# Dilated attention's product groups tied to their last operand, and the exchange's second product moved to the dense PSUM pool

## Chip, cores, metric

One core of a Trainium2 chip runs the whole kernel in one launch. The metric is the device time of the kernel in microseconds (us); the time before is the median of three runs. TensorE is called PE here, VectorE DVE, ScalarE ACT, GpSimd POOL and SyncE SP. A "row" of an instruction order is one instruction, or a run of equal ones.

## The reference

A transformer block over 2048 positions of width 1024, in float32. What matters here is the attention part and the dense products around it (cut):

```python
DILATED_PAIRS = ((128, 1), (512, 4), (2048, 16))     # (window, dilation)

def dilated_branch(q, k, v, slopes, window, dilation):
    ...
    s = jnp.einsum('bdhnqe,bdhnke->bdhnqk', qb, kw).astype(jnp.float32) * (E ** -0.5)
    ...
    s = jnp.where(valid, s + alibi, -jnp.inf)
    m = jnp.max(s, axis=-1, keepdims=True)
    p = jnp.exp(s - m)
    den = jnp.sum(p, axis=-1, keepdims=True)
    o = jnp.einsum('bdhnqk,bdhnke->bdhnqe', p, vw.astype(jnp.float32)) / den
    lse = (m + jnp.log(den))[..., 0]
    ...

def dilated_attention_group(q, k, v):
    ...                                               # the three branches
    weights = jax.nn.softmax(jnp.stack(lses, axis=0), axis=0)
    return jnp.einsum('gbsh,gbshe->bshe', weights, jnp.stack(outs, axis=0))

def reference(...):
    ...
    h = rms_norm(x, norm1_g[l]) * (1 + sc1) + sh1
    proj = h @ w_in[l]                                # input projection
    ...                                               # gated linear attention, dilated attention
    x = x + g1 * (mixed @ w_out[l])
    h = rms_norm(x, norm2_g[l]) * (1 + sc2) + sh2
    u = causal_depthwise_conv(h @ w_up[l], conv_w[l], conv_b[l])
    u_gate, u_val = jnp.split(u, 2, axis=-1)
    x = x + g2 * ((jax.nn.silu(u_gate) * u_val) @ w_down[l])
```

## The kernel before

The 2048 positions are four chunks of 512. Dense products (input projection, output projection, up, down) are each split into three float32r products that add up in one PSUM bank: lines L301, L302 and L303 of `mm3`, 128x512 each, 24 in a row for one output tile of most products and 12 for one of the down projection. A dense product takes its bank from the pool `psg` (four banks, `pg()`), and DVE or ACT reads it out.

Beside this dense work runs the mixing of a chunk: `mix(c)` is two calls of `gla` and four of `attn(c, hp)`, one for each pair of heads. There are 16 calls of `attn` in all, called steps 0 to 15 here (steps 0 to 3 are chunk 0). All of mixing takes its PSUM banks from the pool `psa` (four banks, `pa()`). `run` interleaves the two generators in program order (`beside`): chunk 0's mixing with the input projection, the mixing of chunks 1 to 3 with the output projection and feed-forward part of the chunk before. The order on each engine is then made by a scheduler, which walks its own model of the time and places an instruction on its engine when operands and buffers are ready in that model; each engine executes its rows in that order. A pool gives its buffers out in the order in which the program asks for them.

One step of attention, in the order of the code:

- The scores of the three branches: dilation 16 (L814), 4 and 1 (`scores`, L779, first with `qf`, then with `qn`). A group in `scores` is eight products on four `psa` banks; a bank holds two of them for one head, and the two heads' products alternate. DVE adds the bias and takes the maximum (`TTR`, L785, eight a group); ACT takes the exponentials with their sums (L789, eight a group).
- The exchange, which brings the maxima and sums of the branches to one layout. DVE makes `xm` (L841), PE multiplies it by the constant `x1` (L844, called the x1 product), then a chain of small operations runs on DVE with one exponential on ACT (L846, L847, L849, L851, L852, L853, L854 to L857), which ends in a second `xm` (L860). PE multiplies that by the constant `x4` (L868, the exchange's second product, called the x4 product here). DVE reads it (L870, L871).
- Scaling of the probabilities by DVE (L864 for dilation 4, L875 for dilation 1) and their transposition by PE (`turn`, L799: four transposes into a bank, then one copy by ACT or DVE in turn, L178 and L180); the transposes of dilation 16 stand ahead of the x4 product in the code.
- The products with the values (L896, L901), a last transposition (L916), the sum (L919).

Of the kernel before, what the change touches and what calls it, by code (L numbers as in the profile page):

```python
# [131 lines left out]
class K:  # L132
    def __init__(self, tc, A, ctx):
        self.tc, self.nc, self.A, self.ctx = tc, tc.nc, A, ctx
        pool = lambda name, bufs, **kw: ctx.enter_context(tc.tile_pool(name=name, bufs=bufs, **kw))
        self.const = pool("const", 1)
        self.wraw = pool("wraw", 2)
        self.whi = pool("whi", 4)
        self.wlo = pool("wlo", 4)
        self.hp = pool("hp", 10)  # L140
        self.gp = pool("gp", 5)
        self.xp = pool("xp", 8)
        self.up = pool("up", 2)
        self.tmp = pool("tmp", 2)
        self.at = pool("at", 1)
        self.dr = pool("dr", 1, space=DRAM)
        self.psg = pool("psg", 4, space=PSUM)
        self.psa = pool("psa", 4, space=PSUM)
        self.evac = 0
        self.loads = []  # L150
        self.hist = []

# [10 lines left out]
    def pa(self, name="psa"):  # L163
        return self.psa.tile([P, T], F32, name="psa")

    def pg(self):
        return self.psg.tile([P, T], F32, name="psg")

# [5 lines left out]
    def copy(self, out, in_):  # L174

        self.evac += 1
        if self.evac % 2:
            self.nc.scalar.copy(out, in_)  # L178
        else:
            self.nc.vector.tensor_copy(out, in_)  # L180

    def consts(self):
        nc, A = self.nc, self.A
# [123 lines left out]
    def ada_setup(self):  # L307
        nc, c = self.nc, self.A["c"]
        self.cond = self.const.tile([P, 1024], F32, name="cond")
        nc.sync.dma_start(self.cond, bass.AP(tensor=c.tensor, offset=c.offset, ap=[[0, P], [1, 1024]]))  # L310
        self.n1 = self.cload("norm1_g", [P, KD])
        self.n2 = self.cload("norm2_g", [P, KD])
        self.ba = self.cload("b_ada", [P, 48])
        self.ones = self.const.tile([P, P], F32, name="ones")
        nc.vector.memset(self.ones, 1.0 / 1024)
        self.eps = self.const.tile([P, 1], F32, name="eps")
        nc.vector.memset(self.eps, EPS)
        th = self.at.tile([P, 1024], F32, name="big", bufs=4)
        tanh = nc.scalar.activation(th, self.cond, AF.Tanh, scale=0.5)
        pre = nc.scalar.preload_act_table_set("natural_log_exp_and_others")  # L320
        self.tc.add_manual_dep(pre.ins, tanh.ins.name, mybir.DependencyInfo(mybir.DependencyClass.Sync, mybir.DependencyReason.DATA))
        nc.vector.scalar_tensor_tensor(self.cond, th, 1.0, self.cond, op0=ALU.add, op1=ALU.mult)
        self.mod = self.const.tile([P, 48], F32, name="mod")
        self.G1 = self.const.tile([P, KD], F32, name="G1")
        self.G2 = self.const.tile([P, KD], F32, name="G2")

    def after(self, inst):

# [122 lines left out]
    def proj(self, c, hs, hook=None, done=()):  # L451
# [58 lines left out]
        def wide(b):  # L510

            pss = [self.pg() for _ in range(4)]
            for j in range(4):
                w = self.weights("w_tokw", b, j)
                order = [(i, s) for i in range(2) for s in range(4)]
# [6 lines left out]
                    self.mm3(pss[s], [(h[:, tk], l[:, tk])], w[i:i + 1], i == 0 and j == 0, True)  # L522
                if j < 3:
                    yield
            for s in range(4):
                off = b and put_off
                st = stage("y0" if off else None)
# [213 lines left out]
    def attn(self, c, hp):  # L741
# [30 lines left out]
        def scores(q, key, z0, bias, outs, g):  # L772
# [3 lines left out]
            for i in range(4):  # L776
                z = z0(i)
                for hh in range(2):
                    nc.tensor.matmul(at(i, hh, z), q[H[hh], i * P:(i + 1) * P], key(H[hh], i, z), start=True, stop=True, skip_group_check=True)  # L779
            for i in range(4):  # L780
                z = z0(i)
                for hh in range(2):
                    TTR(outs[hh][:, i, z:], at(i, hh, z), bias[:, z:], mx[:, hh, g, i:i + 1])

        TTR = lambda out, i0, i1, acc: nc.vector.tensor_tensor_reduce(out, i0, i1, 1.0, -3.0e38, ALU.add, ALU.max, acc)  # L785

        def soft(t, hh, g, i, lo, hi):
            h = 2 * hp + hh
# [2 lines left out]
        nm = self.at.tile([P, 2, 3, 4], F32, name="nm", bufs=2)  # L791
        slp = self.C("slp")[:, 24 * hp:24 * hp + 24].rearrange("p (a g i) -> p a g i", a=2, g=3)

        def turn(n, b0, part, to):

            for hh in range(2):
                ps = self.pa()
                for i in range(b0, 4):
                    nc.tensor.transpose(ps[:n, i * P:(i + 1) * P], part(S[hh], i), self.C("id"))  # L799
                self.copy(to(S[hh]), ps[:n, b0 * P:].rearrange("p (r n) -> p r n", n=P))  # L800

        def exps(g, part):

# [57 lines left out]
        for hh in range(2):  # L861
            for i in range(4):
                z = 0 if c else P
                nc.vector.tensor_scalar(s4[hh][:, i, z:], s4[hh][:, i, z:], f[:, hh, 1, i:i + 1], None, op0=ALU.mult)  # L864
        turn(nk, 0, lambda t, i: t[0][:, i * nk:(i + 1) * nk], lambda t: t[0][:nk].rearrange("p (r n) -> p r n", n=P))
        yield
        ps = self.pa()
        nc.tensor.matmul(ps[:, 0:32], self.C("x4"), xm.rearrange("p a b r -> p (a b r)"), start=True, stop=True)  # L868
        xm = self.at.tile(x4, F32, name="xm", bufs=2)[:, 0:2]
        nc.vector.tensor_tensor(xm, ps[:, 0:32].rearrange("p (a b r) -> p a b r", b=4, r=4), self.C("s1")[:, None, None, :].to_broadcast(x2), op=ALU.mult)  # L870
# [1 line left out]
        for hh in range(2):  # L872
            for i in range(4):
                z = 0 if (c or i) else P
                nc.vector.tensor_scalar(sn[hh][:, i, z:], sn[hh][:, i, z:], f[:, hh, 2, i:i + 1], None, op0=ALU.mult)  # L875

        def weigh(out, g):

# [4 lines left out]

        cols = lambda r4, hh: slice((2 * r4 + hh) * 64, (2 * r4 + hh + 1) * 64)
        for z in (P, 0) if c else (P,):
            turn(P, 0, lambda t, i: t[1][:, i, z:z + P], lambda t: t[1][:, :, z:z + P])
        yield
        for z in (P, 0):
            b0 = 0 if (c or z) else 1
            turn(P, b0, lambda t, i: t[2][:, i, z:z + P], lambda t: t[2][:, b0:, z:z + P])  # L890
        yield
        O16 = self.pa()
        for hh in range(2):
# [269 lines left out]
```

## Time and profile before

| | |
|---|---|
| median of the runs | 2615.92 us (2615.84 to 2618.74) |
| profiled execution | 2615.61 us; span of its instructions 2613.8 us |
| busy | PE 98%, DVE 74%, ACT 49%, POOL 17% |
| chain of work that ended last | PE 95% of the span |
| mean granted PE clock | 0.995 |
| DMA | 405.10 MB, mean 155 GB/s |

A row of a group reads: line, engine, operation, tile written and tiles read, sizes, number; then busy time in us and mean ns of one; then the idle time of the engine just before these instructions and what ended it. A row of the timeline reads: start and length in us, engine, line, operation, number of instructions merged, and in brackets the idle time before. A float32 matmul leaves two records in the trace, so eight products stand as x16. Successive matmuls overlap, so a row's length is longer than the step from one start to the next; a step of 0.227 us from one 128x512 product to the next is the dense pace.

### The profile page before, as it was taken

Reading aid. Unit: us, or ns where it says so; the run is one execution under the profiler, and the core shown is the slowest. Engines: PE = TensorE matmul, PEld = TensorE weight load, DVE = VectorE, ACT = ScalarE, POOL = GpSimd, SP = SyncE. Lnnn points to the kernel's source line nnn. Section 1 sums busy time; section 2 is a strip of 40 time slices with the busy share of each in tenths; the row PEclk is TensorE's granted clock in tenths of the full one; section 3 lists DMA queues with packets and bytes.
Section 4 is the critical chain, followed back from the end, with each engine's and each line's share of the span. In section 5 each row is a group of like instructions: output and inputs, shape, how many; then the busy total and the mean of one; then the engine's idle time right before and its main releaser. Section 6 shows DMA issues by size and latency. Waiting matters only on the chain.

```text
span 2613.8 us, 46823 instructions
## 1 busy us (share of the span) xinstructions
PE 2563.5 (98%) x18152; PEld 2105.6 (81%) x18152; DVE 1922.3 (74%) x4075; ACT 1288.8 (49%) x2622; POOL 440.9 (17%) x812
## 2 busy tenths in 40 slices
PE   5999999999999999999999999999999999999999
PEld 3887888788788888887788888878888888788887
DVE  7578886767778777776888777679777775766665
ACT  4566556666554444543555444345445453433332
POOL 1343342312210000012100000310000002200001
PEclk9999999999999999999999999999999999999999
DMA  8766575655632344345423444643344435432222
GB/s 297 254 220 222 186 249 178 212 173 190 236 121 94 114 129 133 120 147 209 141 92 117 140 132 140 241 148 106 115 142 138 134 115 185 153 100 98 97 98 85
DMA packets 164992, 405.10 MB, mean 155 GB/s; under 512 B 19985, under 2 KB 62754, under 8 KB 163490
## 3 DMA queue, kind: packets, MB, share of 16 engines
q0 software_dynamic: 88128, 308.59, 35.1%
q1 hardware_dynamic: 76642, 93.51, 11.3%
q8 instruction: 143, 2.34, 0.4%
q14 instruction: 79, 0.65, 0.1%
HBM read 339.12 MB, written 62.91 MB: 154 GB/s over the span
## 4 chain that ended last, share of the span: by engine, by line
PE 95%; DMA 1%; DVE 1%; ACT 1%; issue 1%; SPq 0%; POOL 0%; POOLq 0%; DVEq 0%; ACTq 0%
PE psg L301 27%; PE psg L302 27%; PE psg L303 27%; PE psa L799 3%; PE psa L779 2%; PE psa L901 2%; PE psa L635 2%; PE psa L896 1%; PE psa L708 1%; PE psa L814 1%; PE psa L707 1%; DVE wada L348 0%; PE psa L712 0%; DMA qf<-q 0%; DMA k_norm_g_sb<-in_k_norm_g_dram 0%
## 5 line engine op out<-in xcount | busy, mean ns | idle before, releaser
L302 PE MATMUL psg<-hlo,whi 128*128 128x512 f32 x1992 | 783.9, 394 | 8.4 <-DVE hlo L447 8.0
L301 PE MATMUL psg<-hhi,whi 128*128 128x512 f32 x1992 | 783.0, 397 | 9.0 <-ACT hhi L445 6.4
L303 PE MATMUL psg<-hhi,wlo 128*128 128x512 f32 x1992 | 781.9, 393 | 0.7 <-DVE wlo L236 0.7
L235 ACT CAST whi<-wraw 128x1024 fp32r<-128x1024 f32 (+1 forms) x391 | 410.5, 1051 | 482.1 <-PE psg L302 386.2
L236 DVE TENSOR_TENSOR wlo<-wraw,whi 128x1024 fp32r<-128x1024 f32 (+1 forms) x391 | 478.2, 1223 | 205.2 <-ACT whi L235 196.5
L301 PEld LDWEIGHTS psg<-hhi,whi 128*128 128x128 f32 x1992 | 375.1, 189 | 96.0 <-ACT hhi L445 12.0
L302 PEld LDWEIGHTS psg<-hlo,whi 128*128 128x128 f32 x1992 | 376.1, 189 | 88.8 <-DVE hlo L447 11.3
L303 PEld LDWEIGHTS psg<-hhi,wlo 128*128 128x128 f32 x1992 | 376.3, 189 | 81.5 <-issue 2.0
L301 PE MATMUL psg<-ghi,whi 128*128 128x512 f32 x744 | 294.3, 397 | 0.1
L302 PE MATMUL psg<-glo,whi 128*128 128x512 f32 x744 | 292.6, 393 | 0.8 <-DVE glo L945 0.8
L303 PE MATMUL psg<-ghi,wlo 128*128 128x512 f32 x744 | 291.8, 392 | 0.7 <-DVE wlo L236 0.7
L229 POOL DMA_DIRECT2D wraw<-in_w_up_dram x176 | 93.2, 529 | 988.5 <-DVE wlo L236 814.3
L1019 DVE SCALAR_TENSOR_TENSOR x<-psg,mod,x 128x512 f32<-128x512 f32 x192 | 143.3, 749 | 118.8 <-PE psg L303 118.3
L301 PE MATMUL psg<-whi,hhi 128*128 128x512 f32 (+2 forms) x512 | 172.4, 344 | 0.6 <-ACT stg L531 0.5
L302 PE MATMUL psg<-wlo,hhi 128*128 128x512 f32 (+2 forms) x512 | 173.0, 339 | 0.0
L303 PE MATMUL psg<-whi,hlo 128*128 128x512 f32 (+2 forms) x512 | 172.6, 341 | 0.0
L301 PEld LDWEIGHTS psg<-ghi,whi 128*128 128x128 f32 x744 | 139.6, 188 | 33.5 <-issue 4.1
L302 PEld LDWEIGHTS psg<-glo,whi 128*128 128x128 f32 x744 | 139.8, 188 | 31.3 <-issue 2.6
L303 PEld LDWEIGHTS psg<-ghi,wlo 128*128 128x128 f32 x744 | 139.7, 188 | 30.4 <-DVE wlo L236 1.1
L789 ACT ACTIVATE big<-big,nm 128x256 f32<-128x256 f32 (+1 forms) x256 | 122.4, 480 | 34.1 <-DVE nm L804 34.1
L974 ACT ACTIVATE y<-psg,conv_b_sb,conv_w_sb 128x512 f32<-128x512 f32 x176 | 136.0, 775 | 3.0 <-PE psg L303 1.7
L975 DVE SCALAR_TENSOR_TENSOR y<-psg,conv_w_sb,y 128x511 f32<-128x511 f32 x176 | 130.7, 743 | 3.0 <-ACT y L974 2.8
(237 smaller groups left out, 3608.4 us busy)
## 6 DMA issues: line engine op xcount, KB each, us to landing
wraw<-in_w_up_dram POOLq DMA_DIRECT2D x176, 512.0 KB, 3.6
wraw<-in_w_down_dram POOLq DMA_DIRECT2D x88, 512.0 KB, 3.6
wraw<-in_w_ch_dram POOLq DMA_DIRECT2D x44, 512.0 KB, 4.4
v<-v SPq DMA_DIRECT2D x68, 256.0 KB, 5.2
wada<-in_w_ada_dram POOLq DMA_DIRECT2D x64, 256.0 KB, 4.6
wraw<-in_w_tokw_dram POOLq DMA_DIRECT2D x32, 512.0 KB, 4.4
wraw<-in_w_out_dram POOLq DMA_DIRECT2D x32, 512.0 KB, 4.8
sq<-in_xT_dram POOLq DMA_DIRECT2D x48, 256.0 KB, 5.0
```

The lines of the kernel that those rows point to most:

```text
L229: self.dq.dma_start(raw[:, :n], src)
L235: nc.scalar.copy(hi[:, :n], raw[:, :n])
L236: nc.vector.tensor_tensor(lo[:, :n], raw[:, :n], hi[:, :n].bitcast(F32), op=ALU.subtract)
L301: nc.tensor.matmul(ps, wh, hh, start=first and k == 0, stop=False, skip_group_check=shared)
L302: nc.tensor.matmul(ps, wh, hl, start=False, stop=False, skip_group_check=shared)
L303: self.lastmm = nc.tensor.matmul(ps, wl, hh, start=False, stop=k == n - 1, skip_group_check=shared)
L635: nc.tensor.matmul(sp[j:j + w, o + n * w:o + (n + 1) * w], kh[R, k0:k0 + w], qh[R, q0:q0 + w], start=True, stop=True)
L789: nc.scalar.activation(t[:, lo:hi], t[:, lo:hi], AF.Exp, bias=nm[:, hh, g, i:i + 1], scale=2.0 ** -(h + 1), accum_out=dn[:, hh, g, i:i + 1])
L799: nc.tensor.transpose(ps[:n, i * P:(i + 1) * P], part(S[hh], i), self.C("id"))
L974: nc.scalar.activation(y, ps, AF.Identity, bias=self.cb[:, b:b + 1], scale=self.cw[:, 2, b:b + 1])
L975: nc.vector.scalar_tensor_tensor(y[:, 1:], ps[:, :T - 1], self.cw[:, 1, b:b + 1], y[:, 1:], op0=ALU.mult, op1=ALU.add)
L1019: nc.vector.scalar_tensor_tensor(x1, ps, self.mod[:, 40 + cb:41 + cb], x1, op0=ALU.mult, op1=ALU.add)
```

## The change

- `tie(inst, to)` adds a dependency: `inst` begins after `to` has completed. The first product of a group in `scores` is tied to the last `TTR` before it. The first transpose of dilation 4's probabilities is tied to the last of their scalings, and the first of dilation 1's to the last of theirs and to the last copy of the transposes before.
- The x4 product takes its bank by `px()`: from `psg`, the dense pool, unless a `wide` product has all four of that pool's banks open at that place of the program; then from `psa` as before.

```diff
+    def px(self):
+
+        return self.pa() if self.wide_open else self.pg()
...
         self.evac += 1
         if self.evac % 2:
-            self.nc.scalar.copy(out, in_)
-        else:
-            self.nc.vector.tensor_copy(out, in_)
+            return self.nc.scalar.copy(out, in_)
+        return self.nc.vector.tensor_copy(out, in_)
...
+    def tie(self, inst, to):
+
+        self.tc.add_manual_dep(inst.ins, to.ins.name, mybir.DependencyInfo(mybir.DependencyClass.Sync, mybir.DependencyReason.DATA))
...
             pss = [self.pg() for _ in range(4)]
+            self.wide_open = True
...
+            self.wide_open = False
...
-                    nc.tensor.matmul(at(i, hh, z), q[H[hh], i * P:(i + 1) * P], key(H[hh], i, z), start=True, stop=True, skip_group_check=True)
+                    mm = nc.tensor.matmul(at(i, hh, z), q[H[hh], i * P:(i + 1) * P], key(H[hh], i, z), start=True, stop=True, skip_group_check=True)
+                    if i == hh == 0:
+
+                        self.tie(mm, last["ttr"])
...
-        TTR = lambda out, i0, i1, acc: nc.vector.tensor_tensor_reduce(out, i0, i1, 1.0, -3.0e38, ALU.add, ALU.max, acc)
+        last = {}
+
+        def TTR(out, i0, i1, acc):
+            last["ttr"] = nc.vector.tensor_tensor_reduce(out, i0, i1, 1.0, -3.0e38, ALU.add, ALU.max, acc)
...
-        def turn(n, b0, part, to):
+        def turn(n, b0, part, to, wait=()):
 
             for hh in range(2):
                 ps = self.pa()
                 for i in range(b0, 4):
-                    nc.tensor.transpose(ps[:n, i * P:(i + 1) * P], part(S[hh], i), self.C("id"))
-                self.copy(to(S[hh]), ps[:n, b0 * P:].rearrange("p (r n) -> p r n", n=P))
+                    tr = nc.tensor.transpose(ps[:n, i * P:(i + 1) * P], part(S[hh], i), self.C("id"))
+                    if wait:
+
+                        for w in wait:
+                            self.tie(tr, w)
+                        wait = ()
+                last["copy"] = self.copy(to(S[hh]), ps[:n, b0 * P:].rearrange("p (r n) -> p r n", n=P))
...
-                nc.vector.tensor_scalar(s4[hh][:, i, z:], s4[hh][:, i, z:], f[:, hh, 1, i:i + 1], None, op0=ALU.mult)
+                last["s4"] = nc.vector.tensor_scalar(s4[hh][:, i, z:], s4[hh][:, i, z:], f[:, hh, 1, i:i + 1], None, op0=ALU.mult)
...
-        ps = self.pa()
+        ps = self.px()
         nc.tensor.matmul(ps[:, 0:32], self.C("x4"), xm.rearrange("p a b r -> p (a b r)"), start=True, stop=True)
...
-                nc.vector.tensor_scalar(sn[hh][:, i, z:], sn[hh][:, i, z:], f[:, hh, 2, i:i + 1], None, op0=ALU.mult)
+                last["sn"] = nc.vector.tensor_scalar(sn[hh][:, i, z:], sn[hh][:, i, z:], f[:, hh, 2, i:i + 1], None, op0=ALU.mult)
...
-            turn(P, 0, lambda t, i: t[1][:, i, z:z + P], lambda t: t[1][:, :, z:z + P])
+            turn(P, 0, lambda t, i: t[1][:, i, z:z + P], lambda t: t[1][:, :, z:z + P], (last["s4"],) if z else ())
...
-            turn(P, b0, lambda t, i: t[2][:, i, z:z + P], lambda t: t[2][:, b0:, z:z + P])
+            turn(P, b0, lambda t, i: t[2][:, i, z:z + P], lambda t: t[2][:, b0:, z:z + P], (last["sn"], last["copy"]) if z else ())
```

In the changed file the lines lie further down: the dense products are L305 to L307, the scores L789, the transposes L815, the x1 product L865 and the x4 product L889, with `xm` from L862 and L881.

How the rows stand, at three places. First PE in step 4 (the first of chunk 1, beside the down projection of chunk 0). The numbers behind a name count the tiles in the order in which the program makes them. Before, around the x1 product `psa_9872`:

```order
L303 MATMUL psg_9915<-ghi_8915,wlo_9719 128x512
L844 MATMUL psa_9872<-xm_9828,consts_sb_442 128x64
L799 MATMUL psa_9897<-consts_sb_442,s16_9546 64x128 x4
L799 MATMUL psa_9903<-consts_sb_442,s16_9547 64x128 x4
L301 MATMUL psg_9915<-ghi_9079,whi_9718 128x512
L302 MATMUL psg_9915<-glo_9081,whi_9718 128x512
L303 MATMUL psg_9915<-ghi_9079,wlo_9719 128x512
L301 MATMUL psg_9966<-ghi_8608,whi_9718 128x512
```

and, 32 dense products after the x1 product, around the x4 product `psa_9929`:

```order
L301 MATMUL psg_10092<-ghi_8758,whi_9786 128x512
L302 MATMUL psg_10092<-glo_8760,whi_9786 128x512
L868 MATMUL psa_9929<-xm_9887,consts_sb_442 128x32
L799 MATMUL psa_9942<-consts_sb_442,big_9674 128x128 x4
L799 MATMUL psa_9948<-consts_sb_442,big_9675 128x128 x3
```

Now:

```order
L307 MATMUL psg_9915<-ghi_9079,wlo_9719 128x512
L865 MATMUL psa_9872<-xm_9828,consts_sb_442 128x64
L815 MATMUL psa_9897<-consts_sb_442,s16_9546 64x128 x4
L815 MATMUL psa_9903<-consts_sb_442,s16_9547 64x128 x4
L889 MATMUL psg_9929<-xm_9887,consts_sb_442 128x32
L305 MATMUL psg_9966<-ghi_8608,whi_9718 128x512
L306 MATMUL psg_9966<-glo_8610,whi_9718 128x512
```

Before, the dense tiles 9966, 10010 and 10092 begin ahead of tile 9929; now 9929 stands in the dense pool's sequence, and 9966 and all later dense tiles begin behind it. Between the x1 and the x4 product there are the eight transposes and no dense product.

Second, PE in step 2 (chunk 0, beside the input projection), from the last scores to the x4 product. Now:

```order
L789 MATMUL psa_5939<-kw_5674,qn_5672 128x256
L789 MATMUL psa_5940<-kw_5674,qn_5672 128x256
L593 MATMUL psa_6036<-consts_sb_442,gl_5630 16x128 x4
L600 MATMUL psa_6044<-gw_459,glr_6041 128x256 x2
L600 MATMUL psa_6053<-gw_459,glr_6041 128x256 x2
L865 MATMUL psa_6065<-xm_6034,consts_sb_442 128x64
L815 MATMUL psa_6090<-consts_sb_442,s16_5716 32x128 x4
L815 MATMUL psa_6096<-consts_sb_442,s16_5717 32x128 x4
L486 MATMUL psa_6148<-sqr_6141,blk_464 128x512
L487 MATMUL psa_6148<-sqr_6142,blk_464 128x512
L889 MATMUL psg_6166<-xm_6080,consts_sb_442 128x32
L305 MATMUL psg_6197<-hhi_5568,whi_5873 128x512
```

Before, the same x1 product stood in the middle of tile 6197, with dense products on both sides:

```order
L301 MATMUL psg_6197<-hhi_5610,whi_5873 128x512
L590 MATMUL psa_6044<-gw_459,glr_6041 128x256 x2
L590 MATMUL psa_6053<-gw_459,glr_6041 128x256 x2
L844 MATMUL psa_6065<-xm_6034,consts_sb_442 128x64
L799 MATMUL psa_6090<-consts_sb_442,s16_5716 32x128 x4
L302 MATMUL psg_6197<-hlo_5612,whi_5873 128x512
L303 MATMUL psg_6197<-hhi_5610,wlo_5874 128x512
```

From the last score to the x1 product 46 dense products stood before and none stands now.

Third, DVE in step 13 (chunk 3, beside the up projection of chunk 2), from the chain's first rows on. Now:

```order
L867 TENSOR_TENSOR xm<-psa,consts_sb 128x64
L868 TENSOR_REDUCE md<-xm 128x4x4
L870 TENSOR_REDUCE M<-md 128x8
L240 TENSOR_TENSOR wlo<-wraw,whi 128x1024
L872 TENSOR_TENSOR f<-md,M 128x24
L184 COPY s_20343<-psa 128x512
L996 SCALAR_TENSOR_TENSOR y_20706<-psg,conv_w_sb,y_20706 128x511
L999 SCALAR_TENSOR_TENSOR y_20706<-halo,conv_w_sb,y_20706 128x1
L1007 SCALAR_TENSOR_TENSOR th<-th,y_20631 128x512
L873 TENSOR_TENSOR f<-f,consts_sb 128x24
```

Before:

```order
L846 TENSOR_TENSOR xm<-psa,consts_sb 128x64
L847 TENSOR_REDUCE md<-xm 128x4x4
L236 TENSOR_TENSOR wlo<-wraw,whi 128x1024
L180 COPY s_20343<-psa 128x512
L849 TENSOR_REDUCE M<-md 128x8
L975 SCALAR_TENSOR_TENSOR y_20631<-psg,conv_w_sb,y_20631 128x511
L978 SCALAR_TENSOR_TENSOR y_20631<-halo,conv_w_sb,y_20631 128x1
L991 TENSOR_TENSOR glo<-y_20585,ghi 128x512
L851 TENSOR_TENSOR f<-md,M 128x24
```

In both, rows that read dense results or split weights stand between the rows of the chain; which ones stand there has shifted by about one dense tile.

More of the change, by code (lines that the diff above doesn't have):

```diff
@@ L524, in wide @@
                     yield
+            self.wide_open = False
             for s in range(4):
```

## The prediction

> **What bounds the kernel now.** I read first the busy times and the shares of the chain that ended last, then the busy time of the long middle of the run, then single steps of attention in the timeline.
>
> ```profile
> PE 2563.5 (98%) x18152; PEld 2105.6 (81%) x18152; DVE 1922.3 (74%) x4075; ACT 1288.8 (49%) x2622; POOL 440.9 (17%) x812
> PE 95%; DMA 1%; DVE 1%; ACT 1%; issue 1%; SPq 0%; POOL 0%; POOLq 0%; DVEq 0%; ACTq 0%
> 400.00:2200.00 1800.00, 1790.05 (x13718) 1465.55 (x13718) 1353.52 (x3132) 915.45 (x2052) 262.32 (x484) 1.00 0.45 148
> ```
>
> PE is the bound. In the 1800 us of the third row (length, then busy time of PE, PEld, DVE, ACT and POOL, granted clock) it stands still for 10 us in all. So a change can win only by making PE's own rows cheaper, up to those 10 us, and every new wait of PE lengthens the run by its whole length, since no slack is left to take it up. PE can be kept busy because the attention's waits are filled with dense products. The question is whether they still are.
>
> The exchange of step 4 shows what is filled (start, length, engine, line):
>
> ```profile
> 937.99 0.33 PE L844 MATMUL psa<-xm,consts_sb 128*128 128x64 f32 x2
> 938.15 1.04 PE L799 MATMUL psa<-consts_sb,s 128*64 128x128 f32 x8
> 939.22 0.22 DVE L846 TENSOR_TENSOR xm<-psa,consts_sb 128x64 f32<-128x64 f32 x1
> 940.04 0.68 DVE L180 COPY s<-psa 64x512 f32<-64x512 f32 x1
> 940.64 0.17 DVE L852 TENSOR_TENSOR f<-f,consts_sb 128x24 f32<-128x24 f32 x1
> 940.74 0.74 DVE L1019 SCALAR_TENSOR_TENSOR x<-psg,mod,x 128x512 f32<-128x512 f32 x1
> 940.84 0.22 ACT L853 ACTIVATE f<-f 128x24 f32<-128x24 f32 x1 [1.47 <-DVE f L852]
> 941.40 0.17 DVE L854 TENSOR_TENSOR md<-md,f 128x24 f32<-128x24 f32 x1
> 942.27 0.20 DVE L860 TENSOR_TENSOR xm<-f,consts_sb 128x32 f32<-128x32 f32 x1
> 942.38 2.19 DVE L864 TENSOR_SCALAR big<-big,f 128x256 f32<-128x256 f32 x8
> 946.31 0.31 PE L868 MATMUL psa<-xm,consts_sb 128*128 128x32 f32 x2
> ```
>
> The x4 product's operand is written by L860, which ends at 942.47, 4.48 us after the x1 product began; the x4 product runs at 946.31. Nobody waits in these 8.3 us, because 32 dense products fill them.
>
> **A. The x4 product in the dense pool: waits.** The pool hands out its buffers in program order. With the x4 product's tile in that sequence, no dense product that comes later in the program may begin before it. In the changed order of PE the dense products between the x1 and the x4 product number, from step 0 to 15: 0, 58, 0, 0, 0, 24, 0, 9, 2, 0, 0, 0, 24, 0, 0, 0; none had fewer than 32 before. Steps 1, 5 and 12 keep cover; in 13 steps PE holds little but the x1 product and eight transposes, 937.99 to 939.19 above, 1.2 us, and then waits. Behind the x4 product in PE's queue stand all the dense rows.
>
> The wait is the latency of the chain less that work. The chain alone: 0.33 us of the x1 product and 942.47 − 939.22 = 3.25 us from L846 to L860 (a copy and an L1019 are in it), 3.6 us. DVE takes its rows in order, and in the changed order more rows stand within the chain: 9 splits of weights, 31 rows of the feed-forward's or projection's read-outs.
>
> ```profile
> L236 DVE TENSOR_TENSOR wlo<-wraw,whi 128x1024 fp32r<-128x1024 f32 (+1 forms) x391 | 478.2, 1223 | 205.2 <-ACT whi L235 196.5 <-PE psg L303 3.2 <-PE psa L479 0.2
> L976 DVE SCALAR_TENSOR_TENSOR y<-psg,conv_w_sb,y 128x510 f32<-128x510 f32 x176 | 130.9, 744 | 0.7
> L986 DVE SCALAR_TENSOR_TENSOR th<-th,y 128x512 f32<-128x512 f32 x88 | 60.7, 689 | 35.9 <-ACT th L985 35.9
> L979 DVE SCALAR_TENSOR_TENSOR y<-halo,conv_w_sb,y 128x2 f32<-128x2 f32 x132 | 28.0, 212 | 0.0
> 1047.64 0.39 PE L301 MATMUL psg<-hhi,whi 128*128 128x512 f32 x1
> 1049.71 0.39 PE L301 MATMUL psg<-hhi,whi 128*128 128x512 f32 x1
> ```
>
> They cost 9 × 1.223 = 11.0, 31 × 0.72 (between the 0.744 and 0.689 of the two middle rows) = 22.3, and seven of L979's kind 1.5: 34.8 us. Between the two PE rows lie nine steps, 0.23 us each; the 11 dense products that stand in steps 7 and 8 cover 2.5 us, two small groups (L478, L479) 0.7. So 13 × 3.6 + 34.8 − 13 × 1.2 − 3.2 = **63 us**. Step by step (0, 2, 3, 4, 6, 7, 8, 9, 10, 11, 13, 14, 15): 7.7, 2.9, 5.6, 2.4, 5.8, 5.2, 5.7, 5.2, 3.6, 2.4, 6.9, 6.9, 2.4. The low end is the chain with none of those rows in its way, 46.8 − 15.6 − 3.2 = 28: once PE stands still it makes nothing new for DVE to read. The high end takes the latencies from the x1 product to the end of L860 as they were in these 13 steps; the first and last:
>
> ```profile
> 439.68 0.33 PE L844 MATMUL psa<-xm,consts_sb 128*128 128x64 f32 x2
> 447.90 0.19 DVE L860 TENSOR_TENSOR xm<-f,consts_sb 128x32 f32<-128x32 f32 x1
> 2134.68 0.33 PE L844 MATMUL psa<-xm,consts_sb 128*128 128x64 f32 x2
> 2142.95 0.19 DVE L860 TENSOR_TENSOR xm<-f,consts_sb 128x32 f32<-128x32 f32 x1
> ```
>
> 8.4 and 8.5 us, 102 over all 13: 102 − 15.6 − 3.2 = 83. I take 63, from the rows as they now stand in DVE's order.
>
> **B. The x1 product: waits.** It moves forward as well, since the x4 product behind it now holds the dense rows. Between the last dilation-1 score and the x1 product stood at least 41 dense products in every step; now step 2 has none, step 9 20, step 10 22, steps 14 and 15 33, the others 42 or more. What they covered is the maximum, the exponentials and L841:
>
> ```profile
> 1606.65 2.00 PE L779 MATMUL psa<-kw,qn 64*128 64x256 f32 x16
> 1618.01 0.23 DVE L841 TENSOR_TENSOR xm<-md,consts_sb 128x64 f32<-128x64 f32 x1 [3.38 <-ACT big L789]
> 563.57 1.14 PE L779 MATMUL psa<-kw,qn 64*128 64x256 f32 x8
> 572.06 0.23 DVE L841 TENSOR_TENSOR xm<-md,consts_sb 128x64 f32<-128x64 f32 x1
> L590 PE MATMUL psa<-gw,glr 17*128 17x256 f32 x32 | 8.0, 387 | 0.0
> ```
>
> From the end of the scores at 1608.65 to 1618.24 are 9.6 us (step 11); in step 2, 564.71 to 572.29, 7.6. Waits: 9.6 − 20 × 0.23 = 5.0; 4.5; twice 2.0; and in step 2 7.6 less some 2.0 of small groups (four products of L590 and four transposes) 5.6. Sum **19 us**. Low: two fewer rows of L236's kind in the way, 2.4 less in each, 8; high: two more in each, 31.
>
> **C. The clock after a wait.** Two waits of PE stand in the trace with what followed:
>
> ```profile
> 617.17 0.88 PE L814 MATMUL psa<-kt,qf 64*32 64x32 f32 x64 [2.89 <-DMA qf<-q]
> 617.20:620.50 3.30, 3.30 (x76) 3.23 (x77) 1.15 (x17) 1.21 (x8) 0.00 (x0) 0.50 0.89 327
> 1748.60 0.26 PE L635 MATMUL psa<-pt 64*32 64x32 f32 x6 [1.90 <-issue]
> 1748.60:1752.00 3.40, 3.40 (x20) 2.80 (x20) 3.40 (x8) 2.34 (x5) 2.65 (x5) 1.00 0.59 174
> ```
>
> After 2.89 us without work the next 3.3 us ran at a granted clock of 0.50, which costs half of them, 1.65 us; after 1.90 us the clock stayed at 1.00. Of the waits above ten of A (2.9 and longer) and three of B are as long as the first: 13 × 1.65 = **21 us**. Low: only the five longest, about twice 2.89 us and more (steps 0, 6, 8, 13 and 14), 8; high: two such stretches for each, 43.
>
> [...]
>
> **D. The ties: groups joined.** Where half a group of scores waited for a bank, dense products stood between the halves; the first product of a tied group waits until all four banks are read, and its eight run together. Step 6 shows both kinds:
>
> ```profile
> 1044.51 1.13 PE L779 MATMUL psa<-kw,qf 64*128 64x256 f32 x8
> 1045.58 0.50 PE L301 MATMUL psg<-hhi,whi 128*128 128x512 f32 x1
> 1045.91 0.40 PE L302 MATMUL psg<-hlo,whi 128*128 128x512 f32 x1
> 1046.24 1.14 PE L779 MATMUL psa<-kw,qf 64*128 64x256 f32 x8
> 1047.30 0.50 PE L303 MATMUL psg<-hhi,wlo 128*128 128x512 f32 x1
> 1052.52 2.00 PE L779 MATMUL psa<-kw,qn 64*128 64x256 f32 x16
> 1054.44 0.50 PE L301 MATMUL psg<-hhi,whi 128*128 128x512 f32 x1
> ```
>
> Start to start, the halves take 1.07 + 1.06 us, the whole 1.92: 0.21 saved. A dense product beside a switch takes 0.33 in place of 0.23, on both sides, which saves another 0.20: 0.41 a join. Runs of scores fall from 51 to 36: nine joins of two halves in chunks 1 to 3 (3.7), one of three pieces (some 0.8 to 1.5), five in chunk 0 (2.0); runs of transposes fall from 92 to 52, priced at 0.8 in all, since joined transposes save the switch alone and many runs only touch other attention rows. Sum **−8 us**, bounds −4 (scores of chunks 1 to 3) and −12 (a 0.10 switch on every transposes' join too). The ties themselves make no new wait: before dilation 4's transposes stand 21 to 27 dense products, at least 4.8 us, against eight scalings that take 2.19 us together (the L864 row), and 22 to 33 more before dilation 1's. POOL, SP and the DMAs they issue keep their order but for small shifts; DMA queues are not what PE waits for.
>
> **Sum.** 63 + 19 + 21 − 8 = +95 to the profiled execution's 2615.6 us (0.3 under the median): about 2711 us. I take 2712.
>
> **Rivals.**
> The queue drains. While PE stands still, DVE may already be through the rows that I put into the chain, and only the lone chain is left: A 28, B 8, C 12 (waits of 2.4 us lie midway between 1.90 and 2.89, so half of 13 fall), D −8: +40, 2656 us. For it: DVE is busy 74% only; against: those rows stand ahead of the chain's in DVE's own order and read products that PE ends just before it waits.
> The clock stays low. Each wait costs two half-clock stretches, and the latencies are the measured ones: 83 + 19 + 43 − 8 = +137, 2753 us. For it: two waits a step lie within 10 us of each other.
> Other side: the chain is ready before the eight transposes end. That needs a latency under about 1.2 us at each x4 product; then A and C vanish, B with them, and D's −8 is left: 2608 us. The shortest latency in the trace is step 4's 4.48, so little speaks for it.
> The change does nothing: the bank's pool rarely limits and the moved products cost and save alike, 2616 us. The order speaks against it.
>
> **How the numbers follow.** The forecast has 0.64, the drained queue 0.17, the low clock 0.12, the faster rival 0.04, no effect 0.03. About 0.2% (5 us) is what a measurement of this kernel can tell from no change. Only the last two cases are not slower, so faster is 0.04, same 0.03, slower 0.93. The ends: all lows with the largest saving give 28 + 8 + 8 − 12 = +32, all highs 83 + 31 + 43 − 4 = +153; these seldom come together, so I cut to 2655 (the drained queue still in) and 2760 (the low clock still in).
>
> **What would show it.** A: idle time of PE before the x4 product (L889) of 2 to 8 us in 13 steps, released by DVE's L881, and none in steps 1, 5 and 12. B: idle time before the x1 product (L865) in steps 2, 9, 10, 14, 15 alone. C: granted clock 0.50 for about 3.3 us behind the longer waits, and a mean below the 0.995 of now. D: fewer and longer runs of scores, no idle time before the tied transposes. The forecast is wrong if the x4 waits sum to under 30 us, if dense rows are found between the x1 and the x4 product, or if a wait appears at the transposes or at the scores that the tie makes.

## The result and the profile after

The changed kernel takes 2733.51 us (median of 4 runs, 2733.09 to 2734.21) against 2616.3 for the kernel before on the same chip: a ratio of 1.0445, 95% interval 1.0432 to 1.0458. The profiled execution is at 2733.24 us, its span 2731.5 us, 117.7 more than before. One run of the kernel with the transposes tied alone, further down, took 3632.53 us at a granted clock of 0.655 and is left out of that kernel's median and ratio.

The page's busy times and shares of the chain that ended last, and the middle of the run (start and end, length, busy time of PE, PEld, DVE, ACT and POOL, granted clock, DMA share, GB/s):

```profile
PE 2596.5 (95%) x18152; PEld 2130.3 (78%) x18152; DVE 1931.2 (71%) x4075; ACT 1286.3 (47%) x2623; POOL 440.7 (16%) x812
PE 69%; issue 15%; DVE 8%; ACT 6%; DMA 2%; POOL 1%; SPq 0%; POOLq 0%; DVEq 0%; ACTq 0%
400.00:2300.00 1900.00, 1804.53 (x13654) 1475.15 (x13653) 1354.00 (x3121) 907.78 (x2044) 252.28 (x466) 0.97 0.42 137
```

PE stands still for 95 of these 1900 us, where it stood for 10 of 1800 before, and its busy time has grown although the number of its instructions is the same. The first is waiting, the second is a slower clock: 0.97 in the middle, 0.973 over the run. PE's own waits name the places (engine, line, what was waited for, us in all, times, longest):

```profile
PE psg L889 <- DVE xm L881: 61.6, 13, 7.7
PE psa L865 <- DVE xm L862: 18.9, 5, 6.5
```

The first is the x4 product waiting for the end of the chain on DVE, the second the x1 product waiting for `xm`. Neither place is among PE's waits before. Step 14 shows both, PE first and then DVE:

```profile
2161.10 0.43 PE L865 MATMUL psa<-xm,consts_sb 128*128 128x64 f32 x2 [3.04 <-DVE xm L862]
2161.37 1.12 PE L815 MATMUL psa<-consts_sb,s 128*128 128x128 f32 x8
2168.63 0.64 PE L889 MATMUL psg<-xm,consts_sb 128*128 128x32 f32 x2 [6.14 <-DVE xm L881]
```

```profile
2161.57 0.22 DVE L867 TENSOR_TENSOR xm<-psa,consts_sb 128x64 f32<-128x64 f32 x1 [0.53 <-PE psa L865]
2161.97 1.22 DVE L240 TENSOR_TENSOR wlo<-wraw,whi 128x1024 fp32r<-128x1024 f32 x1
2163.10 0.17 DVE L870 TENSOR_REDUCE M<-md 128x8 f32<-128x24 f32 x1
2163.19 0.68 DVE L184 COPY s<-psa 128x512 f32<-128x512 f32 x1
2163.79 0.68 DVE L1012 TENSOR_TENSOR glo<-y,ghi 128x512 fp32r<-128x512 f32 x1
2164.39 0.74 DVE L996 SCALAR_TENSOR_TENSOR y<-psg,conv_w_sb,y 128x511 f32<-128x511 f32 x1
2165.18 0.17 DVE L872 TENSOR_TENSOR f<-md,M 128x24 f32<-128x24 f32 x1
...
2166.89 0.69 DVE L1007 SCALAR_TENSOR_TENSOR th<-th,y 128x512 f32<-128x512 f32 x1 [0.66 <-ACT th L1006]
2168.39 0.19 DVE L881 TENSOR_TENSOR xm<-f,consts_sb 128x32 f32<-128x32 f32 x1
```

Between the x1 and the x4 product PE has the eight transposes and then nothing. On DVE the chain's short rows (L867, L870, L872, L881) are strung out between long rows that have nothing to do with it: a split of weights (L240), the feed-forward's read-outs (L996, L1012, L1007). DVE takes them in its order, so the chain is done 7.5 us after the x1 product began.

The clock in the same step, in five stretches of 3.41 us one behind the other, called windows below:

```profile
2158.79:2162.20 3.41, 1.10 (x10) 1.08 (x10) 1.39 (x5) 3.41 (x12) 0.00 (x0) 1.00 0.45 154
2162.20:2165.61 3.41, 0.29 (x2) 0.00 (x0) 3.41 (x8) 1.24 (x3) 0.53 (x1) 0.50 0.23 53
2165.61:2169.03 3.42, 0.40 (x2) 0.40 (x3) 2.62 (x12) 0.80 (x3) 0.00 (x0) 0.50 0.25 101
2169.03:2172.44 3.41, 3.41 (x10) 2.73 (x10) 3.34 (x15) 0.00 (x0) 0.00 (x0) 0.50 0.00 0
2172.44:2175.85 3.41, 3.41 (x16) 2.74 (x16) 0.78 (x3) 0.00 (x0) 0.00 (x0) 1.00 0.02 5
```

The second figure is PE's busy time. In the first stretch PE is busy for 1.10 of 3.41 us and the clock falls behind it. It is still at 0.50 in the fourth, in which PE works throughout (8 dense products begin in it, 14 in the fifth; the step from one to the next is 0.43 us there and 0.23 in the fifth), and comes back only after that one.

The whole difference, taken apart. Idle time is the span less PE's busy time; the clock loss is an estimate from these steps and the granted clock, half of PE's busy time in the stretches at 0.50; the work is what is left of the busy time.

| profiled execution | span | PE idle | clock loss | work |
|---|---|---|---|---|
| before | 2613.8 | 50.3 | 11.4 | 2552.1 |
| after | 2731.5 | 135.0 | 48.4 | 2548.0 |
| difference | +117.7 | +84.7 | +37.0 | −4.1 |

Of the 84.7 us that PE idles more, 61.6 + 18.9 = 80.5 stand ahead of the two products.

### The profile page after: what moved, and what is told of

Its sections match the earlier page's. It is cut to its first block, busy times and chain, and to the rows that moved or that the text cites. A ratio compares the mean times of both kernels' runs of the same rounds, so it can differ in the third digit from the quotient of the medians.

```text
span 2731.5 us, 46770 instructions
## 1 busy us (share of the span) xinstructions
PE 2596.5 (95%) x18152; PEld 2130.3 (78%) x18152; DVE 1931.2 (71%) x4075; ACT 1286.3 (47%) x2623; POOL 440.7 (16%) x812
## 4 chain that ended last, share of the span: by engine, by line
PE 69%; issue 15%; DVE 8%; ACT 6%; DMA 2%; POOL 1%; SPq 0%; POOLq 0%; DVEq 0%; ACTq 0%
PE psg L305 20%; PE psg L306 20%; PE psg L307 20%; ACT big L805 2%; DVE wlo L240 2%; PE psa L922 2%; PE psa L815 2%; DVE big L801 1%; PE psa L645 1%; POOL wraw L233 1%; ACT whi L239 1%; PE psa L789 1%; ACT s L805 1%; PE psa L917 0%; PE psa L718 0%
## 5 line engine op out<-in xcount | busy, mean ns | idle before, releaser
L305 PE MATMUL psg<-hhi,whi 128*128 128x512 f32 x1992 | 792.8, 402 | 12.4 <-ACT hhi L453 7.4
L307 PE MATMUL psg<-hhi,wlo 128*128 128x512 f32 x1992 | 788.0, 396 | 1.0 <-DVE wlo L240 1.0
L240 DVE TENSOR_TENSOR wlo<-wraw,whi 128x1024 fp32r<-128x1024 f32 (+1 forms) x391 | 478.2, 1224 | 244.4 <-ACT whi L239 233.1
L305 PEld LDWEIGHTS psg<-hhi,whi 128*128 128x128 f32 x1992 | 381.0, 192 | 101.1 <-ACT hhi L453 14.7
L307 PEld LDWEIGHTS psg<-hhi,wlo 128*128 128x128 f32 x1992 | 380.8, 191 | 85.5 <-issue 3.0
L305 PE MATMUL psg<-ghi,whi 128*128 128x512 f32 x744 | 296.9, 400 | 0.3 <-DVE x L972 0.3
L307 PE MATMUL psg<-ghi,wlo 128*128 128x512 f32 x744 | 293.7, 395 | 1.6 <-DVE wlo L240 1.6
L307 PE MATMUL psg<-whi,hlo 128*128 128x512 f32 (+2 forms) x512 | 171.8, 340 | 0.0
L305 PE MATMUL psg<-whi,hhi 128*128 128x512 f32 (+2 forms) x512 | 171.3, 342 | 0.0
L305 PEld LDWEIGHTS psg<-ghi,whi 128*128 128x128 f32 x744 | 141.5, 190 | 32.8 <-issue 3.6
L307 PEld LDWEIGHTS psg<-ghi,wlo 128*128 128x128 f32 x744 | 141.4, 190 | 32.7 <-DVE wlo L240 2.0
L996 DVE SCALAR_TENSOR_TENSOR y<-psg,conv_w_sb,y 128x511 f32<-128x511 f32 x176 | 130.8, 743 | 2.2 <-ACT y L995 2.2
```

What stands on the lines that cost most here:

```text
L240: nc.vector.tensor_tensor(lo[:, :n], raw[:, :n], hi[:, :n].bitcast(F32), op=ALU.subtract)
L305: nc.tensor.matmul(ps, wh, hh, start=first and k == 0, stop=False, skip_group_check=shared)
L307: self.lastmm = nc.tensor.matmul(ps, wl, hh, start=False, stop=k == n - 1, skip_group_check=shared)
L996: nc.vector.scalar_tensor_tensor(y[:, 1:], ps[:, :T - 1], self.cw[:, 1, b:b + 1], y[:, 1:], op0=ALU.mult, op1=ALU.add)
```

## The experiments

Each is a change to the changed kernel. The times are medians, the ratios against the kernel before on the same chip.

**The ties alone.** The x4 product gets its bank from the attention pool again.

```diff
-        ps = self.px()
+        ps = self.pa()
```

> The ties kept, the x4 product back on a bank of the attention pool. Theory (the dense pool's sequence makes the waits, the ties only join groups): at least 34 dense products stand again between the x1 and the x4 product and 36 ahead of the x1 product, so no idle time at either, a mean granted clock of 0.995, and the joined groups' saving alone, 5 us measured in the changed kernel: about 2611 us (2607 to 2614). Rival (the ties make waits of their own, hidden in the changed kernel behind the larger ones): idle time of PE at the first score products or at the tied transposes, 2616 us or more.

Measured: 2619.51 us, ratio 1.0002 (0.9992 to 1.0011).

```profile
PE psa L889 <- DVE xm L881: 0.7, 1, 0.7
```

The waits are gone but for one of 0.7 us. The time is in the range of the rival, not of the theory: two of 12 runs only reached the 2611 us expected (2611.27 and 2611.65, both at a granted clock of 0.995; the longest took 2623.56 at 0.991). But the wait that the rival needs, at the scores or the tied transposes, is not seen. PE's work is 2544.4 us, 7.7 less than before, and yet the run isn't shorter: the profiled one has 6.3 us more idle time and 1.7 more clock loss, in small pieces at other places. Why they come with the ties is open.

**The bank alone.** No ties, the x4 product in the dense pool.

```diff
-                        self.tie(mm, last["ttr"])
+                        pass
...
-            turn(P, 0, lambda t, i: t[1][:, i, z:z + P], lambda t: t[1][:, :, z:z + P], (last["s4"],) if z else ())
+            turn(P, 0, lambda t, i: t[1][:, i, z:z + P], lambda t: t[1][:, :, z:z + P])
...
-            turn(P, b0, lambda t, i: t[2][:, i, z:z + P], lambda t: t[2][:, b0:, z:z + P], (last["sn"], last["copy"]) if z else ())
+            turn(P, b0, lambda t, i: t[2][:, i, z:z + P], lambda t: t[2][:, b0:, z:z + P])
```

> The x4 product in the dense pool, no ties. Its order on PE has 0 to 6 dense products between the x1 and the x4 product in steps 0, 2, 3, 4, 10, 11, 14 and 15 and 24 or more in the others, and at least 32 ahead of every x1 product. Theory: waits at the x4 product in these eight steps alone, by the changed kernel's waits less 0.23 us for each dense product 30 us, none at the x1 product, half-clock losses in proportion (38 x 8/18 = 17), no joins: 2616 + 47 = 2663 us (2645 to 2680). Rival (the bank alone makes the whole loss, the ties are only a saving of 5): 2739 us.

Measured: 2691.02 us, ratio 1.0278 (1.0264 to 1.0291).

```profile
PE psg L889 <- DVE xm L881: 41.5, 10, 7.5
PE psg L889 <- ACT halo L1002: 4.2, 1, 4.2
PE psg L889 <- ACT whi L239: 0.9, 1, 0.9
```

The time is outside the range expected, and the truth lies between theory and rival: the bank makes 74 us of the 117; the ties, which cost nothing alone, bring the rest once the bank is there. In steps 6, 7, 8 and 13 the order here keeps 24, 32, 24 and 24 dense products between the two products, with the ties 0, 9, 2 and 0; why the ties move them is not shown. The x1 product waits nowhere, as expected. The waits at the x4 product are 46.6 us in 12 steps, and not 30 in eight (the two rows that name ACT are steps 13 and 8, in which L881 too ends only 0.15 us before the x4 product). The largest miss is a reading: step 9, which I had counted among those with 24 or more dense products, has none and waits 7.49 us. Steps 8, 12 and 13 have 24 ahead and still wait 0.93, 1.79 and 4.20. The experiment with the x4 product one place later shows how that can be.

**The bank opened early.** A small product of constants into the same bank stands ahead of the x4 product and waits for nothing of the chain.

```diff
+        nc.tensor.matmul(ps[:, 0:32], self.C("x4"), self.C("b4")[:, 0:32], start=True, stop=True)
         nc.tensor.matmul(ps[:, 0:32], self.C("x4"), xm.rearrange("p a b r -> p (a b r)"), start=True, stop=True)
```

> The changed kernel, with one more small product (128x32, of constants) into the x4 product's bank ahead of it; it waits for nothing of the chain, so the bank is given out early. Theory (dense products were held because a pool hands out its buffers in program order and the x4 product's was not handed out before the chain ended): 28 or more dense products stand between the x1 and the x4 product again, no idle time there, the joins are kept, 16 small products cost 1 to 2 us: about 2613 us (2609 to 2620). Rival (a dense bank is lost to the chain, and three are too few for the dense products): no idle time at the x4 product, but idle time of PE at dense products, 2640 us or more. If the waits stay, 2733 us.

Measured: 2614.70 us, ratio 0.9991 (0.9982 to 0.9999). PE's page row and its rows in step 15 (dense products left out):

```profile
PE 2557.0 (98%) x18184; PEld 2108.7 (81%) x18184; DVE 1921.6 (74%) x4075; ACT 1284.5 (49%) x2623; POOL 440.1 (17%) x812
2137.91 0.33 PE L865 MATMUL psa<-xm,consts_sb 128*128 128x64 f32 x2
2138.08 1.04 PE L815 MATMUL psa<-consts_sb,s 128*128 128x128 f32 x8
2149.66 0.31 PE L890 MATMUL psg<-xm,consts_sb 128*128 128x32 f32 x2
```

The x4 product comes 11.8 us after the x1 product without a wait. It sits in the dense pool as in the changed kernel and the ties are there; the only difference is that its bank is handed out early. So the 117 us are the price of a bank that stood next in the pool's sequence and could not be taken, and a dense bank held during the chain costs nothing that shows.

**The wait filled.** Eight products of constants (128x256) in a bank of the attention pool run ahead of the x4 product.

```diff
+FILL = 8
...
+        fill = self.pa()
+        for i in range(FILL):
+            nc.tensor.matmul(fill[:, 0:256], self.C("x4"), self.C("b4"), start=True, stop=True, skip_group_check=True)
         ps = self.px()
```

> The changed kernel with eight products of constants (128x256, 3.4 us together) in a bank of the attention pool ahead of the x4 product, so that PE works through most of each wait. Theory (the clock falls because PE is idle for half of a window): the x4 waits shrink from 62 us to about 15, the loss at half clock from 38 us to about 15; the products cost 3.4 us in each of the steps that had no wait (1, 5, 12) or get dense cover in this order (6 and 13, 12 us of waits gone): 2733 + 17 - 12 - 5 - 20 = about 2713 us. Rival (the clock falls for another reason than idle time): loss at half clock stays near 38, 2735 us or more.

Measured: 2715.96 us, ratio 1.0382 (1.0369 to 1.0395).

```profile
PE psa L868 <- DVE xm L865: 14.4, 4, 6.5
PE psg L895 <- DVE xm L884: 12.5, 6, 4.7
```

The time is as expected, 18 us below the changed kernel's. In the profiled run, the longest of the four (2724.15 us), PE's work grows by the 54.9 us of the added products (16 steps of 3.4) and the idle time falls by 55.8, so these two cancel, and what the run gains is clock loss. The x4 waits fall to 12.5 us as expected, but not by the filling alone: in this order 24 dense products stand ahead of the x4 product in steps 6 and 13 and 42 ahead of the x1 product in step 2, which takes away 12.2 and 4.5 us of waits. The clock loss fell less than I said, from 48.4 to 40.2, so this run alone doesn't decide. The same kernel was run once more (its label wrongly says that ties are missing; they are there):

> The filled wait once more, to see how the run's clock goes with its place in the 3.41 us grid: the same order of instructions, 2714 to 2725 us and a mean granted clock of 0.984 to 0.988; the profiled run's loss at half clock between 28 and 42 us, the higher the lower its clock. Rival (the loss is fixed by the order): the same 40 us.

Measured: 2713.04 us, one run, clock 0.988. Idle time 82.3 us and work 2601.5 are close to those of the first run (79.2 and 2602.9), the clock loss is 27.4 in place of 40.2, just below the range expected. The order of instructions is the same, so "fixed by the order" falls. Step 10 shows what differs. Its x1 product waits 3.62 us in the first run and 3.65 in the second. Three windows of 3.41 us of each run, the first run's above:

```profile
1620.50:1623.91 3.41, 1.02 (x5) 0.52 (x3) 1.62 (x5) 3.13 (x13) 0.00 (x0) 1.00 0.25 98
1623.91:1627.32 3.41, 2.19 (x10) 2.12 (x11) 1.65 (x4) 2.43 (x6) 0.00 (x0) 0.50 0.00 0
1627.32:1630.74 3.42, 3.42 (x10) 2.70 (x10) 2.96 (x14) 0.22 (x1) 0.53 (x1) 0.50 0.42 152
1613.18:1616.59 3.41, 0.08 (x1) 0.08 (x1) 0.70 (x2) 3.41 (x14) 0.00 (x0) 1.00 0.00 0
1616.59:1620.00 3.41, 3.41 (x14) 3.07 (x15) 2.63 (x7) 1.19 (x3) 0.53 (x1) 0.50 0.00 0
1620.00:1623.42 3.42, 3.42 (x18) 3.04 (x17) 3.09 (x14) 0.16 (x1) 0.00 (x0) 1.00 0.47 153
```

In the first run the wait lies across two windows and costs two at half clock; in the second it fills one and costs one. Both losses are below the 48.4 of the unfilled kernel. In the eleven steps that keep as many dense products ahead of the x4 product as the unfilled order (all of the 13 but 6 and 13), the time at half clock falls from 99 us to 51 and 38, as it must if the idle time makes it.

**One place later.** The x4 product's code, with what reads it and the scaling of dilation 1, stands behind the transposes of dilation 4 and their `yield` (the diff is cut to what it comes to).

```diff
-        ps = self.px()
-        nc.tensor.matmul(ps[:, 0:32], self.C("x4"), xm.rearrange("p a b r -> p (a b r)"), start=True, stop=True)
...
             turn(P, 0, lambda t, i: t[1][:, i, z:z + P], lambda t: t[1][:, :, z:z + P], (last["s4"],) if z else ())
         yield
+        ps = self.px()
+        nc.tensor.matmul(ps[:, 0:32], self.C("x4"), xm.rearrange("p a b r -> p (a b r)"), start=True, stop=True)
...
```

> The changed kernel with the x4 product's code one place later in the program, behind the transposes of dilation 4, so that about one more dense tile is asked for ahead of its bank. Its order on PE has 0, 65, 0, 23, 11, 36, 48, 26, 26, 2, 0, 7, 48, 26, 21 and 0 dense products between the x1 and the x4 product and at least 29 ahead of every x1 product. Theory (the dose: exactly the dense tiles that the program asks for earlier are what covers the wait, 0.23 us each): of the changed kernel's waits 7.7, 4.9, 1.2, 3.6, 2.5, 1.7, 1.3 and 4.2 us are left in steps 0, 2, 4, 9, 10, 11, 14 and 15, 27 us in all, none at the x1 product; half-clock losses in proportion, 13 to 17; joins kept, -4: about 2655 us (2640 to 2670). Rival (the place in the program does not matter, a dense bank alone makes the waits): 2733 us.

Measured: 2667.78 us, ratio 1.0191 (1.0174 to 1.0208). The place in the program decides, and more than half of the loss goes with one place. But the waits are 43.4 us and not 27:

```profile
PE psg L900 <- DVE xm L881: 43.4, 9, 8.7
2178.36 0.33 PE L865 MATMUL psa<-xm,consts_sb 128*128 128x64 f32 x2
2188.23 0.64 PE L900 MATMUL psg<-xm,consts_sb 128*128 128x32 f32 x2 [8.66 <-DVE xm L881]
2181.35 0.21 DVE L867 TENSOR_TENSOR xm<-psa,consts_sb 128x64 f32<-128x64 f32 x1
2187.98 0.19 DVE L881 TENSOR_TENSOR xm<-f,consts_sb 128x32 f32<-128x32 f32 x1
```

That is step 15, where I had carried over the changed kernel's 4.15 us. There one other row (0.68 us) stood between L867 and L881; here eight do, 5.16 us, and from the start of the x1 product to the end of L881 pass 9.81 us in place of 5.42. Step 14 waits 5.18 us in place of 1.3 in the same way. I had kept the latency and only subtracted the cover. Moving the dense products also moves their read-outs and splits on DVE, and some of them come to stand in the chain. In the run with the bank alone step 13 is the same: 24 dense products ahead, 13 other rows of 8.3 us in the chain.

**The ties one kind at a time**, with the x4 product in the attention pool. Both kernels start from that with the ties alone; the first leaves out the ties at the transposes (the two lower pairs of lines of the diff of the bank alone), the second those at the scores:

```diff
-                        self.tie(mm, last["ttr"])
+                        pass
```

> Only the ties at the scores; x4 product in the attention pool, transposes untied. Runs of score products on PE 36 (51 before), runs of transposes 103 (92 before). Theory (the prices of the prediction: 0.41 us for each joined group of scores, next to nothing for transposes): PE's work apart from idle time and half clock falls by 6 to 7 of the 7.7 us that both ties saved. Rival (what counts is each switch between dense and attention rows, some 0.2 us): the dense products stand in 323 runs, 331 before, so it falls by 2 us. The time is within 0.2% of before either way.

> Only the ties at the transposes; x4 product in the attention pool, scores untied. Runs of transposes on PE 61 (92 before), of score products 51 as before, of dense products 303 (331 before). Theory (the prediction's prices): PE's work falls by about 1 us. Rival (each switch counts, some 0.2 us): by 5 to 6 us. The time is within 0.2% of before either way.

Measured: score ties 2612.13 us, ratio 0.9979 (0.9970 to 0.9989); transpose ties 2615.91 us over nine runs, 0.9998 (0.9988 to 1.0007). PE's work falls by 3.7 and by 4.5 us, together 8.2, with both 7.7. Neither set of prices holds: the score ties save some half of the 6 to 7 us expected, the transpose ties four to five times what I had given them, nearer to the rival. The prices aren't cleanly apart either, since with the score ties alone the runs of transposes rise from 92 to 103. The score ties alone are the fastest of all kernels here, 5 us below the kernel before, just at what can be told from no change.

**The opened bank without ties, and with score ties alone.** Both add the small opening product; the first has all three pairs of lines of the diff of the bank alone, the second its two lower ones.

> The x4 product in the dense pool with the small opening product ahead of it, no ties: 27 or more dense products between the x1 and the x4 product in every step. Theory: the bank alone, once it is opened early, costs and saves next to nothing: no idle time at the x4 product, 2615 to 2620 us. Rival (three dense banks are too few while the chain runs): idle time of PE at dense products, 2625 us or more.

> The ties at the scores alone, the x4 product in the dense pool with its small opening product: 28 or more dense products between the x1 and the x4 product in every step, 36 runs of scores, 68 of transposes. Theory (score ties save some 4 us, the bank opened early costs and saves nothing): no idle time at the x4 or x1 product and 2612 us (2608 to 2616), as with the score ties alone. Rival (the freed attention bank is worth something once scores are joined): 2608 us or less.

Measured: 2617.51 us, ratio 0.9999 (0.9990 to 1.0009), and 2617.85 us, 1.0003 (0.9994 to 1.0012). The first is as expected, with no idle time at dense products beyond that of before: the opened bank costs and brings nothing. The second missed both theories: work is down by 5.9 us, but idle time is up by 4.9 and clock loss by 5.3. So a saving of this size in PE's work does not reliably reach the end of the run, and the opened bank is no improvement to carry on.

## Why the prediction was right, point by point

**A, waits at the x4 product: right.** 63 us predicted, 61.6 measured, in the 13 steps named and in no other. The term of 34.8 us for other DVE rows was read from their order alone. In these 13 steps other rows take 43.3 us between L867 and L881, of which 13 copies of 0.68 (L184) were already in the base: 34.5. That the whole sum came so close is luck all the same, for two errors cancel. From the start of the x1 product to the end of L881 pass 89.5 us in the 13 steps, where the sum has 46.8 + 34.8 = 81.6: it gave 0.33 us to the way from the x1 product to L867, and DVE still has other rows there, so that this way takes 19.4 us in all and not 4.3. Step 15, whose x1 product begins at 2243.95:

```profile
2244.60 1.23 DVE L240 TENSOR_TENSOR wlo<-wraw,whi 128x1024 fp32r<-128x1024 f32 x1 [0.71 <-ACT whi L239]
2245.75 0.75 DVE L1040 SCALAR_TENSOR_TENSOR x<-psg,mod,x 128x512 f32<-128x512 f32 x1
2246.41 0.21 DVE L867 TENSOR_TENSOR xm<-psa,consts_sb 128x64 f32<-128x64 f32 x1
```

Against that PE's work between the two products is 24.9 us, and 4.1 more are waits ahead of other rows, where the sum has 15.6 + 3.2 = 18.8 of cover: the x1 product and the eight transposes take 2.39 us in place of 1.2 in steps 9 and 10, where the clock is at 0.50. The rival of the drained queue (28 us) falls: those rows were ahead of the chain's in DVE's order and ran there whether PE waited or not. (Its C should read 11 us and not 12, half of 13 falls of 1.65 us, which changes nothing.) Single steps were less exact, by 1.2 us in the mean. Step 3 waits 0.76 us here and not 5.6, since 3.25 of it are taken ahead of a small group (L486) that stands in the gap; step 2 has 4.87 and not 2.9, step 15 4.15 and not 2.4, step 9 4.01 and not 5.2.

**B, waits at the x1 product: right.** 19 predicted, 18.9 measured, in the five steps named: 4.46, 6.48, 3.65, 3.04 and 1.26 in steps 2, 9, 10, 14 and 15, against 5.6, 5.0, 4.5, 2.0 and 2.0. Here too the single errors, about 1 us each, cancel in the sum.

**C, the clock: the mechanism right, the term mis-sized.** 21 predicted, 37 measured. The failed step is "13 × 1.65": one half-clock stretch of 3.3 us for each wait of 2.9 us or more. There are 13 stretches, but only by chance the 13 forecast: one in each of the 13 steps, in which two waits can share a stretch. And they are far longer, 3.4 to 17.1 us. The traces show something else. In the profile after, all 39 changes of the clock, from 49.35 to 2728.81 us, lie within 0.005 us of one grid of 3.4133 us, and so do the 13 of the profile before. What the clock did behind a window of that grid goes with PE's idle time in it. Counted over the windows behind 100 us of twelve profiles, by the share of the window in which PE was idle:

| clock in the window | PE idle | windows | clock falls or stays low behind it |
|---|---|---|---|
| 1.00 | under 0.3 | 8646 | 16 |
| 1.00 | 0.3 to 0.5 | 57 | 13 |
| 1.00 | 0.5 and more | 74 | 72 |
| 0.50 | under 0.005 | 97 | 3 |
| 0.50 | 0.005 to 0.1 | 15 | 8 |
| 0.50 | 0.1 and more | 52 | 52 |

So half a window without work was followed by a fall in 72 of 74 cases, 0.3 to 0.5 of one in 13 of 57 (the 16 falls behind busier windows the table does not explain). The clock came back behind 94 of 97 windows of all but unbroken work (under 0.5% idle time), with up to 10% of idle time in 7 of 15, with more in none of 52. A window at half clock with 10% of idle time or more, such as one late in which a wait ended, was followed by another one each time (52 of 52), and where a second wait came within the stretch, as x4's follows x1's, the stretch grew. Step 14 above has 10.24 us at half clock from waits of 3.04 and 6.14 us, the longest stretch (step 2) 17.07. The 13 stretches of the attention's steps took 116 us, with PE busy for 70 of them; half of that, 35 us, stands where the prediction has 21.
The rival of the low clock (two stretches a wait, 43 us) was nearer on this term, but its waits of 83 us were not; its 2753 us lies about as far above the 2733 measured as my 2712 does below.

**D, the joins: right in sign, small.** −8 predicted, −4.1 measured in PE's work, within the bounds of −4 to −12. The prices were wrong: tied alone, the transposes bring as much as the scores, 4.5 us against the 0.8 that they were priced at. In the profile before, the first dense product behind a run of transposes takes 0.315 us from start to start in the median of 69, against the dense pace of 0.227, so each switch less saves some 0.09 us there. With the transposes tied alone the dense products stand in 28 runs less, which makes an estimated 2.5 of the 4.5 us; the rest is open. The ties made no wait of their own that the traces show, as said.

**The rivals without a loss** fall by A's waits; and the reason given, that the pool's sequence holds the dense products back, is what the early opening shows by taking the whole loss away. The sum came out 21 us short: C 16, D 4, other idle time 4 (84.7 less 80.5), less 3 for A, B and rounding.

## What to carry to other kernels

A scheduler that fills an engine's waits can only do so with work whose buffers are handed out. When a late result is given a buffer from the pool that the filling work uses, everything behind it in the program waits for the late result, though it needs nothing of it; ask, for every new tenant of a pool, when its first write can run, and open the buffer early with a small write or leave the tenant where it was.
A wait can be worked out beforehand from the order of rows on the engines and the durations of another run, if the rows of other work that stand inside the chain are counted, not the chain alone; and they must be counted anew for every version.

## What the runs showed of the hardware that was not expected

The table of windows above: a fall after half an idle window (72 of 74), a return behind all but unbroken ones (94 of 97 with under 0.5% idle time, none of 52 with 10% or more). With it comes a spread that no instruction order explains: the same kernel with the filled waits lost 40.2 us to the clock in one run and 27.4 in another. In step 10 the same wait of 3.6 us cost 6.83 us at half clock in the one and 3.41 in the other, by where it fell in the grid; the other steps were not taken apart like that.
